# High and low activations as one 512-column operand: three matmuls of 256 columns become one of 512 and one of 256

## The chip, the cores and the metric

One core of a Trainium2 chip runs the whole program in one launch. The metric is the device time in microseconds (us); lower is better. The engines that matter here are TensorE (matmuls, "PE" in the profile, its weight loads "PEld"), VectorE ("DVE"), ScalarE ("ACT"), GpSimd ("POOL") and SyncE ("SP"), which issues the DMAs of the weights.

## The reference, cut to what matters

Two transformer blocks of depth 2 each run over 256 tokens of width 1024. The first block has a mixer with three branches (differential attention, windowed attention, a short convolution), cross attention to a memory of 256 tokens, and a gated network with a convolution of three taps; the second has two gated networks around a mixer. Nearly all the arithmetic is `x @ w` with float32 weights. The gated networks show the form:

```python
def conv_ffn(x, ffn_w_in, ffn_conv_w, ffn_conv_b, ffn_w_out):
    u, gt = jnp.split(x @ ffn_w_in, 2, axis=-1)
    a = dwconv(gt, ffn_conv_w) + ffn_conv_b
    return (jax.nn.silu(a) * u) @ ffn_w_out
...
def swiglu(x, wg, wu, wd):
    return (jax.nn.silu(x @ wg) * (x @ wu)) @ wd
```

Here x is [256, 1024], the inner width is 2816, that is 22 blocks of 128 features.

## The kernel before

**Numbers.** Each float32 value v is held as a pair: a high part h (v rounded to the matmul's format, `F32R`) and a low part v - h. A product is the sum of three matmuls: weight high x activation high, weight high x activation low, weight low x activation high.

**Weights.** They are packed on the host in the order of their use, in halves of [128, 1024]. For each half SyncE issues one DMA of 512 KB into one of 5 staging buffers (`dma_w`, line 296), ScalarE copies it into a high buffer (`split_h`, line 306, 8 buffers), and VectorE subtracts to get the low part (`split_l`, line 318, 7 buffers), which frees the staging buffer and lets the next DMA be issued. `take(key, part)` is called for each half in turn, and calls `pump`, which emits the splits up to 4 halves ahead (low parts) and 5 ahead (high parts). All of this is written out in program order, and each engine runs its instructions in that order.

**Two forms of product.** In form A (`half_A`, `chunk_A`) a [128, 128] weight tile is the stationary operand and the activations xT, [128 features, (high, low), 256 tokens], are the moving one; the result is [128 features, 256 tokens]. One half holds 8 such tiles, one for each slice of the contraction, so it has 8 x 3 = 24 matmuls. A chunk is two halves, whose results lie side by side in one bank of [128, 512]. In the forms B and BK (`group_B`, `group_Bt`, `run_BK`, lines 421 to 501) the activations are stationary and 512 columns of weights move. The change touches form A alone: the keys of cross attention, q and k of the windowed attention, the convolution's projections, the gates and branches of the first mixer, the queries of cross attention, and the up and gate products of all gated networks ("UG", 18 chunks in `ffn1`, 20 in each `swiglu`). In the branches ("A4") a half holds two results of 4 slices each.

**Banks.** Four banks in pool `acc`, four in pool `tp`. The last two chunks of a gated network take theirs from `tp`, since the product behind it needs all four of `acc`.

**Steps.** After each half, `step()` emits work that runs beside the products: attention stages (`attend`), the angle table (`small_setup2`), deferred functions. In `ffn1` the function `gated(j, g, u)` emits for each chunk one activation on ScalarE (line 1238), two multiply-adds on VectorE (1239 and 1240), and, one step later, an activation (1243), a product (1244) and the split of the result (513 on ScalarE, 514 on VectorE). In `swiglu` each chunk has one activation (1336), one product (1337) and the same split. At the start of `ffn1` the chunks c = 0 and 1 ("ffg") have two `gated` each.

Of the kernel before, what the change touches and what calls it, by code (L numbers as in the profile page):

```python
# [11 lines left out]
F32 = mybir.dt.float32  # L12
# [16 lines left out]
HOLD = 4  # L29
NHL = 8  # L30
# [66 lines left out]
def pack_weights(I):  # L97
    """Lays the weights out block by block in the order of their use."""
# [25 lines left out]
    for e in ORDER:  # L124
# [47 lines left out]
# columns of the packed per-feature parameters  # L172
# [16 lines left out]
def pack_rpb(I):  # L189
    """[layer, pair of heads, query, head, key row offset, key column] by index."""  # L190
# [7 lines left out]
def constants():  # L198
    """Tables that the shapes alone determine."""
# [31 lines left out]
class Gen:  # L231
    def __init__(self, nc, tc, T, ctx):
# [9 lines left out]
        self.p_sm = P("sm", 24)  # L242
        PS = bass.MemoryType.PSUM
# [39 lines left out]
    def tp(self):  # L283
        """One of four banks; those of a step are read at the start of the next one."""
# [38 lines left out]
    def pump(self, upto, ahead=1):  # L323
        """High parts up to upto + 1, low parts up to upto."""
# [56 lines left out]
    def mm3(self, out, lh, ll, rh, rl, start, stop):  # L381
        mm = self.nc.tensor.matmul
        mm(out, lh, rh, start=start, stop=False)  # L383
        mm(out, lh, rl, start=False, stop=False)  # L384
        mm(out, ll, rh, start=False, stop=stop)  # L385

    def half_A(self, key, part, out, x, nk=8):
        """out [128 features, 256 tokens]; x(k) gives the pair of k."""
        h, l = self.take(key, part)
        for s in range(8 // nk):  # L390
            for k in range(nk):
                c = (s * nk + k) * 128
                xp = x(k)
                self.mm3(out[:, s, :] if nk < 8 else out, h[:, c:c + 128], l[:, c:c + 128], xp[:, 0, :], xp[:, 1, :],
                         k == 0, k == nk - 1)
# [33 lines left out]
    def group_Bt(self, keys, x, between):  # L429
        """As group_B, with all of token tile 0 ahead of tile 1, whose transposes between() emits."""  # L430
# [109 lines left out]
    def ln_chain(self, xs, g, b):  # L540
        """Layer norm of the two halves xs in place, in parts: what follows each half, and the rest."""
# [16 lines left out]
    def rms_chain(self, xs, g):  # L558
        """As ln_chain, into temporaries."""
# [17 lines left out]
    def both_chain(self, xs, g, b, rg):  # L577
        """Layer norm in place, and the rms norm of it."""
# [8 lines left out]
    def turn_half(self, t, c, half, xT):  # L587
        """half [128 tokens, 512] into xT[:, 4c:4c + 4, :, t]; returns what is left: the low part."""
# [19 lines left out]
    def norm_end(self, keys, x, comb, rows, chain, last=TURN_LAST):  # L608
        """run_BK, the residual, the norm and the transposes of tile 0; returns xT and what is left to do for tile 1."""
# [34 lines left out]
    def turn1(self, halves, xT, late=False):  # L644
        """The transposes of tile 1: f(0) and f(1) by halves unless they come late, f() all that is left."""
# [130 lines left out]
    def mm3_rows(self, outs, rows, q, k, t):  # L776
        """Scores of token tile t: row half i of the pairs q and k into outs[i]."""
# [6 lines left out]
    def heads_unit(self, qT, kT, v, bias, nk, dst, vc, done=None, split=False):  # L784
        """Two heads of 64: qT, kT [128 (two heads), 256], pairs where split; v[kt] [128, cols]; dst their pair."""
# [41 lines left out]
    def first(self, ctx):  # L827
# [21 lines left out]
        self.trig = pf.tile([128, 4, 2, 8], F32, name="trig")  # L849
# [31 lines left out]
        for l in range(DEPTH):  # L881
            xT, tr1 = self.mixer1(l, xT, tr1, pna)
            xT, tr1 = self.cross(l, xT, tr1)
            if l == 0:
                self.sides.append(self.small_setup2())
# [705 lines left out]
```

## Time and profile before

| | us |
|---|---|
| runs, median of 3 | 2078.1 |
| runs, lowest and highest | 2074.76 and 2079.68 |
| profiled execution, span from first to last instruction | 2072.1 |
| TensorE busy in it | 2048.7 |
| VectorE busy | 1302.9 |
| ScalarE busy | 1091.0 |

No time of the profiled execution as a whole stands beside its span; the runs' median is 6.0 us above it. TensorE's granted clock is 0.997 of full speed over the span. Busy time is the union of the instructions on an engine. Matmuls are pipelined, so the duration of one contains the start of the next; the distance between starts tells what one costs in a stream.

### The profile page before, as it was taken

The numbers are of one execution on the slowest core, as the hardware profiler recorded it, in microseconds if no ns is written. First come the engines' busy times: TensorE is split into PE (matmuls) and PEld (weight loads), VectorE is DVE, ScalarE is ACT, GpSimd is POOL, SyncE is SP. The second block draws the span as 40 slices with busy tenths as digits, with TensorE's granted clock in tenths as the row PEclk, the third lists the DMA queues.
The fourth block names the chain that finished last, engine by engine and source line by source line (L and its number), as shares of the span: only waits on it lengthen the run. The fifth ranks groups of instructions, "written<-read, shape, count | busy, mean of one in ns | idle before, by whom it ended". The sixth has DMA issues, their size and how long they took to land.

```text
span 2072.1 us, 34809 instructions
## 1 busy us (share of the span) xinstructions
PE 2048.7 (99%) x14064; PEld 1859.9 (90%) x14064; DVE 1302.9 (63%) x2001; ACT 1091.0 (53%) x1798; POOL 97.0 (5%) x142
## 2 busy tenths in 40 slices
PE   8999999999999999999999999999999999999998
PEld 7899988899888999989987998879998998879996
DVE  6776674887577657457766555776554555676553
ACT  5657445465275644536543544575444544574442
POOL 2100000000010000000001000100000000100000
PEclk9999999999999999999999999999999999999999
DMA  8545664466464465545574656445564656545561
GB/s 290 184 151 169 200 209 135 145 207 217 165 203 138 168 204 180 186 133 188 185 240 160 202 191 218 157 160 169 191 217 142 207 187 217 160 151 178 189 215 66
DMA packets 105523, 376.89 MB, mean 182 GB/s; under 512 B 12561, under 2 KB 12817, under 8 KB 105233
## 3 DMA queue, kind: packets, MB, share of 16 engines
q1 hardware_dynamic: 99936, 357.85, 51.8%
q0 software_dynamic: 5136, 16.29, 2.7%
q8 instruction: 110, 1.80, 0.3%
q10 hardware_dynamic: 288, 0.52, 0.1%
q14 instruction: 53, 0.43, 0.1%
HBM read 372.49 MB, written 1.05 MB: 180 GB/s over the span
## 4 chain that ended last, share of the span: by engine, by line
PE 95%; DVE 3%; issue 1%; ACT 1%; POOL 0%; DMA 0%; SPq 0%; POOLq 0%; DVEq 0%
PE acc L383 17%; PE acc L384 17%; PE acc L385 17%; PE acc L476 6%; PE acc L478 6%; PE acc L477 6%; PE acc L501 5%; PE acc L421 3%; PE acc L423 3%; PE acc L422 3%; PE acc L450 1%; PE acc L443 1%; PE acc L445 1%; PE tp L385 1%; PE tp L383 1%; PE tp L384 1%
## 5 line engine op out<-in xcount | busy, mean ns | idle before, releaser
L318 DVE TENSOR_TENSOR wl<-stg,wh 128x1024 fp32r<-128x1024 f32 x670 | 801.5, 1224 | 196.5 <-PE acc L477 128.4
L306 ACT CAST wh<-stg 128x1024 fp32r<-128x1024 f32 (+1 forms) x673 | 683.3, 1047 | 185.4 <-PE acc L478 133.4
L383 PE MATMUL acc<-xT,wh 128*128 128x256 f32 x2624 | 739.5, 282 | 0.6 <-ACT xT L595 0.6
L384 PE MATMUL acc<-xT,wh 128*128 128x256 f32 x2624 | 735.0, 280 | 0.7 <-DVE xT L596 0.7
L385 PE MATMUL acc<-xT,wl 128*128 128x256 f32 x2624 | 734.9, 280 | 0.0
L383 PEld LDWEIGHTS acc<-xT,wh 128*128 128x128 f32 x2624 | 493.8, 188 | 3.3 <-ACT xT L595 1.1
L384 PEld LDWEIGHTS acc<-xT,wh 128*128 128x128 f32 x2624 | 493.9, 188 | 1.7 <-DVE xT L596 1.1
L385 PEld LDWEIGHTS acc<-xT,wl 128*128 128x128 f32 x2624 | 493.7, 188 | 0.0
L476 PE MATMUL acc<-wh,ring 128*128 128x512 f32 x528 | 212.1, 402 | 0.0
L478 PE MATMUL acc<-wh,ring 128*128 128x512 f32 x528 | 208.3, 395 | 0.2
L477 PE MATMUL acc<-wl,ring 128*128 128x512 f32 x528 | 207.2, 392 | 0.0
L478 PEld LDWEIGHTS acc<-wh,ring 128*128 128x128 f32 x528 | 99.1, 188 | 26.6 <-DVE ring L517 1.1
L477 PEld LDWEIGHTS acc<-wl,ring 128*128 128x128 f32 x528 | 99.2, 188 | 22.8
L501 PE MATMUL acc<-wh,ring 128*128 128x512 f32 x384 | 119.6, 399 | 0.0
L476 PEld LDWEIGHTS acc<-wh,ring 128*128 128x128 f32 x528 | 99.1, 188 | 22.6 <-issue 0.3
L1337 DVE TENSOR_TENSOR tmp<-acc,tmp 128x256 f32<-128x256 f32 x72 | 30.5, 424 | 133.9 <-ACT tmp L1336 133.9
L1336 ACT ACTIVATE tmp<-acc 128x256 f32<-128x256 f32 x72 | 27.7, 385 | 161.6 <-PE acc L385 161.6
L513 ACT CAST ring<-tmp 128x256 fp32r<-128x256 f32 x136 | 54.7, 406 | 87.3 <-DVE tmp L1244 42.0
L514 DVE TENSOR_TENSOR ring<-tmp,ring 128x256 fp32r<-128x256 f32 x136 | 57.3, 425 | 64.1 <-ACT ring L513 64.1
L501 PEld LDWEIGHTS acc<-wh,ring 128*128 128x128 f32 x384 | 72.1, 188 | 16.7
L537 POOL TENSOR_TENSOR sm<-sm,mhalf 128x1 f32<-128x1 f32 (+1 forms) x40 | 31.6, 790 | 1046.4 <-DVE sm L548 418.1
L421 PE MATMUL acc<-wh,xT 128*128 128x512 f32 (+1 forms) x192 | 75.3, 392 | 0.0
(235 smaller groups left out, 2652.3 us busy)
## 6 DMA issues: line engine op xcount, KB each, us to landing
stg<-in_wpack SPq DMA_DIRECT2D x673, 512.0 KB, 4.1
nab<-in_rpb POOLq DMA_DIRECT2D x8, 384.0 KB, 3.7
ring<-in_ln_g POOLq DMA_DIRECT2D x12, 256.0 KB, 3.5
ring<-in_ln_b POOLq DMA_DIRECT2D x12, 256.0 KB, 4.6
ring<-in_ffn_norm POOLq DMA_DIRECT2D x8, 256.0 KB, 4.1
cst<-hpad POOLq DMA_DIRECT2D x32, 32.9 KB, 3.8
ring<-in_memT SPq DMA_DIRECT2D x4, 256.0 KB, 5.9
xn<-in_x SPq DMA_DIRECT2D x4, 256.0 KB, 7.2
```

The costliest lines, as they stand in the source:

```text
L306: self.nc.scalar.copy((h.bitcast(F32) if f32 else h)[:, c:c + w], self.stg[i][:, c:c + w])
L318: (self.nc.gpsimd if i in POOL_LOW else self.nc.vector).tensor_sub(l, s, self.hl[i][0].bitcast(F32))
L383: mm(out, lh, rh, start=start, stop=False)
L384: mm(out, lh, rl, start=False, stop=False)
L385: mm(out, ll, rh, start=False, stop=stop)
L421: mm(o, xp[:, 0, ts], h[:, w], start=(i == 0), stop=False)
L422: mm(o, xp[:, 0, ts], l[:, w], start=False, stop=False)
L423: mm(o, xp[:, 1, ts], h[:, w], start=False, stop=(i == n - 1))
L476: mm(b[t][c], xp[:, 0, ts], h[:, w], start=(i == 0), stop=False)
L477: mm(b[t][c], xp[:, 0, ts], l[:, w], start=False, stop=False)
L478: mm(b[t][c], xp[:, 1, ts], h[:, w], start=False, stop=False)
L501: mm(b[tt][cc], xp[:, 1 if kind == "x" else 0, ts], l[:, w] if kind[0] == "l" else h[:, w], start=False, stop=(kind == "x" and i == n - 1))
```

## The change

In form A the high and the low activations of one slice, which lie next to each other in xT, pass as one moving operand of 512 columns over the high weights; the low weights meet the high activations in a second matmul, which adds into the second half of the bank. The bank then holds weight high x activation high in columns 0 to 255, and the other two terms in 256 to 511. A new function `join` adds the two: ScalarE copies the second half into the destination in SBUF, and VectorE adds the first half to it. So each half (each result of 4 slices in the branches) fills a bank of its own. Consumers that read the bank before now read an SBUF tile, `jn` (a new pool of 2) where no other tile was at hand. The angle table `trig` moves into a buffer of the pool of attention biases `nab`. The comments go.

```diff
-    def mm3(self, out, lh, ll, rh, rl, start, stop):
+    def half_A(self, h, l, c, x, nk, pool):
+        ps = pool()
+        p3 = ps.rearrange("p (a b) -> p a b", a=2)
         mm = self.nc.tensor.matmul
-        mm(out, lh, rh, start=start, stop=False)
-        mm(out, lh, rl, start=False, stop=False)
-        mm(out, ll, rh, start=False, stop=stop)
...
+        for k in range(nk):
+            xp = x(k)
+            w = slice(c + k * 128, c + k * 128 + 128)
+            mm(ps, h[:, w], xp.rearrange("p a b -> p (a b)"), start=(k == 0), stop=False)
+            mm(p3[:, 1, :], l[:, w], xp[:, 0, :], start=False, stop=(k == nk - 1))
+        return p3
+
+    def join(self, out, p3):
+        self.nc.scalar.copy(out, p3[:, 1, :])
+        self.nc.vector.tensor_tensor(out, p3[:, 0, :], out, op=ALU.add)
 
-    def chunk_A(self, key, x, step=True, pool=None):
-        ps = (pool or self.acc)()
-        p3 = ps.rearrange("p (a b) -> p a b", a=2)
+    def chunk_A(self, key, x, outs, step=True, pool=None):
         for s in range(2):
-            self.half_A(key, s, p3[:, s, :], x)
+            h, l = self.take(key, s)
+            self.join(outs[s], self.half_A(h, l, 0, x, 8, pool or self.acc))
             if step:
                 self.step()
-        return p3
...
-            ps = self.chunk_A(("A", "xa_k", l, c), lambda k: self.memT[:, k, :, :])
-            self.nc.scalar.copy(self.KT[:, 2 * c:2 * c + 2, :], ps)
+            self.chunk_A(("A", "xa_k", l, c), lambda k: self.memT[:, k, :, :], [self.KT[:, 2 * c + s, :] for s in range(2)])
...
-                    ps = self.chunk_A(("A", "gate%d" % i, l, 2 * c + j), x)
                     g = self.tmp([128, 2, 256])
-                    nc.scalar.activation(g, ps, AF.Sigmoid)
+                    self.chunk_A(("A", "gate%d" % i, l, 2 * c + j), x, self.two(g))
+                    nc.scalar.activation(g, g, AF.Sigmoid)
...
-                    ps = self.acc().rearrange("p (a b) -> p a b", a=2)
-                    self.half_A(("A4", "br%d" % i, l, c), j, ps, ys[i], nk=4)
+                    ps = self.jn()
+                    w = self.take(("A4", "br%d" % i, l, c), j)
+                    for s in range(2):
+                        self.join(ps[:, s, :], self.half_A(w[0], w[1], 512 * s, ys[i], 4, self.acc))
...
-            ps = self.chunk_A(("UG", "ffn", l, j), x, pool=self.acc if j < NFF - 2 else self.tp)
+            ps = self.jn()
+            self.chunk_A(("UG", "ffn", l, j), x, self.two(ps), pool=self.acc if j < NFF - 2 else self.tp)
             gated(j, ps[:, 1, :], ps[:, 0, :])
```

The other callers of `chunk_A` change in the same manner; in the convolution's first projection the copy out of the bank (`gc`) goes, as the sum is written there.

## Rows read from the trace of the kernel before

**Rows 1.** The page's head and its busy time: engine, us, share, instructions.
```profile
span 2072.1 us, 34809 instructions
PE 2048.7 (99%) x14064; PEld 1859.9 (90%) x14064; DVE 1302.9 (63%) x2001; ACT 1091.0 (53%) x1798; POOL 97.0 (5%) x142
```
**Rows 2.** TensorE's waits by cause: us in total, times, longest.
```profile
PE acc L383 <- ACT wh L306: 5.4, 1, 5.4
PE tp L591 <- DVE tmp L573: 2.7, 1, 2.7
PE acc L385 <- DVE wl L318: 1.4, 1, 1.4
...
PE tp L803 <- DVE sm L739: 0.3, 1, 0.3
```
**Rows 3.** Groups of line 383 by shape: count | busy us, mean ns.
```profile
L383 PE MATMUL acc<-xT,wh 128*128 128x256 f32 x2624 | 739.5, 282 | 0.6 <-ACT xT L595 0.6
...
L383 PEld LDWEIGHTS acc<-xT,wh 128*128 128x128 f32 x2624 | 493.8, 188 | 3.3 <-ACT xT L595 1.1
...
L383 PE MATMUL acc<-ring,wh 128*128 128x256 f32 x192 | 54.4, 283 | 0.0
...
L383 PE MATMUL tp<-xT,wh 128*128 128x256 f32 x192 | 53.7, 280 | 0.0
...
L383 PE MATMUL acc<-memT,wh 128*128 128x256 f32 x128 | 38.1, 298 | 5.5 <-ACT wh L306 5.4
```
**Rows 4.** TensorE's timeline, second block's first gated network: start us, us.
```profile
1141.54 0.36 PE L383 MATMUL acc<-xT,wh 128*128 128x256 f32 x1
...
1248.63 0.40 PE L476 MATMUL acc<-wh,ring 128*128 128x512 f32 x1
```
**Rows 5.** TensorE's timeline in the full-width product behind it.
```profile
1262.64 0.40 PE L476 MATMUL acc<-wh,ring 128*128 128x512 f32 x1
...
1285.74 0.40 PE L476 MATMUL acc<-wh,ring 128*128 128x512 f32 x1
```
**Rows 6.** Groups on ScalarE and VectorE by shape: count | busy us, mean ns | idle.
```profile
L513 ACT CAST ring<-tmp 128x256 fp32r<-128x256 f32 x136 | 54.7, 406 | 87.3 <-DVE tmp L1244 42.0 <-DVE tmp L1337 39.5 <-DVE tmp L1117 5.7
...
L1337 DVE TENSOR_TENSOR tmp<-acc,tmp 128x256 f32<-128x256 f32 x72 | 30.5, 424 | 133.9 <-ACT tmp L1336 133.9
...
L1336 ACT ACTIVATE tmp<-acc 128x256 f32<-128x256 f32 x72 | 27.7, 385 | 161.6 <-PE acc L385 161.6
...
L1238 ACT ACTIVATE tmp<-acc,cols 128x256 f32<-128x256 f32 x40 | 22.5, 563 | 29.7 <-PE acc L385 25.0 <-DVE tmp L1240 4.7
...
L513 ACT CAST ring<-tp 128x256 fp32r<-128x256 f32 x48 | 17.8, 370 | 39.9 <-PE tp L1177 17.3 <-PE tp L803 9.2 <-PE tp L1326 6.4
```
**Rows 7.** VectorE's timeline in ffn1 of layer 0, one chunk.
```profile
442.77 0.48 DVE L1239 SCALAR_TENSOR_TENSOR tmp<-acc,cols,tmp 128x255 f32<-128x255 f32 x1
...
446.04 1.22 DVE L318 TENSOR_TENSOR wl<-stg,wh 128x1024 fp32r<-128x1024 f32 x1
447.18 0.48 DVE L1239 SCALAR_TENSOR_TENSOR tmp<-acc,cols,tmp 128x255 f32<-128x255 f32 x1
```
**Rows 8.** Timelines of TensorE and VectorE in ffn1 of layer 0.
```profile
392.52 0.37 PE L383 MATMUL acc<-xT,wh 128*128 128x256 f32 x1
...
413.42 0.48 DVE L1239 SCALAR_TENSOR_TENSOR tmp<-acc,cols,tmp 128x255 f32<-128x255 f32 x1
...
458.17 0.48 DVE L1239 SCALAR_TENSOR_TENSOR tmp<-acc,cols,tmp 128x255 f32<-128x255 f32 x1 [1.13 <-ACT tmp L1238]
```
**Rows 9.** The same in ffn1 of layer 1.
```profile
944.35 0.37 PE L383 MATMUL acc<-xT,wh 128*128 128x256 f32 x1
...
963.25 0.48 DVE L1239 SCALAR_TENSOR_TENSOR tmp<-acc,cols,tmp 128x255 f32<-128x255 f32 x1
```
**Rows 10.** All waits: us in total, times, longest.
```profile
ACT tmp L1336 <- PE acc L385: 161.6, 68, 2.5
...
ACT tmp L1238 <- PE acc L385: 25.0, 22, 1.2
```

More of the change, by code (lines that the diff above doesn't have):

```diff
@@ L29 @@
 HOLD = 4
+JN = 2
 NHL = 8
@@ L242, in __init__ @@
         self.p_sm = P("sm", 24)
+        self.p_jn = P("jn", JN)
         PS = bass.MemoryType.PSUM
@@ L378, in drain, with jn, two @@
             self.step()
-    def mm3(self, out, lh, ll, rh, rl, start, stop):
+    def half_A(self, h, l, c, x, nk, pool):
+        ps = pool()
+        p3 = ps.rearrange("p (a b) -> p a b", a=2)
         mm = self.nc.tensor.matmul
-        mm(out, lh, rh, start=start, stop=False)
-        mm(out, lh, rl, start=False, stop=False)
-        mm(out, ll, rh, start=False, stop=stop)
[L387 to L395, printed above, removed]
-    def chunk_A(self, key, x, step=True, pool=None):
-        ps = (pool or self.acc)()
-        p3 = ps.rearrange("p (a b) -> p a b", a=2)
+        for k in range(nk):
[8 more added lines that the diff above has]
+    def chunk_A(self, key, x, outs, step=True, pool=None):
         for s in range(2):
-            self.half_A(key, s, p3[:, s, :], x)
+            h, l = self.take(key, s)
+            self.join(outs[s], self.half_A(h, l, 0, x, 8, pool or self.acc))
             if step:
                 self.step()
-        return p3
+    def jn(self):
+        return self.p_jn.tile([128, 2, 256], F32, tag="jn", name=self.nm("jn"))
+    def two(self, t):
+        return [t[:, 0, :], t[:, 1, :]]
     def group_B(self, keys, x, step=True, ncol=512):
@@ L848, in first @@
         load_x(1)
-        self.trig = pf.tile([128, 4, 2, 8], F32, name="trig")
         self.posf = pf.tile([128, 2], F32, name="posf")
@@ L884, in first @@
             if l == 0:
+                t = pna.tile([128, 2, 384], F32, tag="nab", name=self.nm("nab"))
+                self.trig = t[:, 0, :64].rearrange("p (a b c) -> p a b c", a=4, b=2)
                 self.sides.append(self.small_setup2())
@@ L1065, in mixer1 @@
             for n, lst, scale in (("qb", qbT, 0.125), ("kb", kbT, 1.0)):
-                ps = self.chunk_A(("A", n, l, c), x)
+                ps = self.jn()
+                self.chunk_A(("A", n, l, c), x, self.two(ps))
                 for s in range(2):
@@ L1104, in mixer1 @@
         for c in range(2):
-            ps = self.chunk_A(("A", "gc", l, c), x)
             gc = self.tmp([128, 2, 256])
-            nc.scalar.copy(gc, ps)
-            ps = self.chunk_A(("A", "hc", l, c), x)
+            self.chunk_A(("A", "gc", l, c), x, self.two(gc))
+            ps = self.jn()
+            self.chunk_A(("A", "hc", l, c), x, self.two(ps))
             nc.vector.tensor_tensor(gc, ps, gc, op=ALU.mult)
@@ L1115, in mixer1 @@
                 nc.vector.scalar_tensor_tensor(y[:, s, :255], gc[:, s, 1:], w(2), y[:, s, :255], op0=ALU.mult, op1=ALU.add)
-            ps = self.chunk_A(("A", "gb", l, c), x)
+            ps = self.jn()
+            self.chunk_A(("A", "gb", l, c), x, self.two(ps))
             nc.vector.tensor_tensor(y, ps, y, op=ALU.mult)
@@ L1134, in mixer1 @@
                 for j in range(2):
-                    ps = self.chunk_A(("A", "gate%d" % i, l, 2 * c + j), x)
                     g = self.tmp([128, 2, 256])
-                    nc.scalar.activation(g, ps, AF.Sigmoid)
+                    self.chunk_A(("A", "gate%d" % i, l, 2 * c + j), x, self.two(g))
+                    nc.scalar.activation(g, g, AF.Sigmoid)
                     gs.append(g)
                 for j in range(2):
-                    ps = self.acc().rearrange("p (a b) -> p a b", a=2)
-                    self.half_A(("A4", "br%d" % i, l, c), j, ps, ys[i], nk=4)
+                    ps = self.jn()
+                    w = self.take(("A4", "br%d" % i, l, c), j)
+                    for s in range(2):
+                        self.join(ps[:, s, :], self.half_A(w[0], w[1], 512 * s, ys[i], 4, self.acc))
                     self.step()
@@ L1195, in q @@
         def q(h):
-            ps = self.chunk_A(("A", "xa_q", l, h), x)
+            ps = self.jn()
+            self.chunk_A(("A", "xa_q", l, h), x, self.two(ps))
             t = self.ring([128, 2, 256])
@@ L1271, in ffn1 @@
         for c in range(2):
-            g = self.chunk_A(("A", "ffg", l, c), x)
+            g = self.jn()
+            self.chunk_A(("A", "ffg", l, c), x, self.two(g))
             for s in range(2):
@@ L1275, in ffn1 @@
         for j in range(4, NFF):
-            ps = self.chunk_A(("UG", "ffn", l, j), x, pool=self.acc if j < NFF - 2 else self.tp)
+            ps = self.jn()
+            self.chunk_A(("UG", "ffn", l, j), x, self.two(ps), pool=self.acc if j < NFF - 2 else self.tp)
             gated(j, ps[:, 1, :], ps[:, 0, :])
@@ L1331, in swiglu @@
         for j in range(2, NFF):
-            ps = self.chunk_A(("UG", n, l, j), x, pool=self.acc if j < NFF - 2 else self.tp)
+            ps = self.jn()
+            self.chunk_A(("UG", n, l, j), x, self.two(ps), pool=self.acc if j < NFF - 2 else self.tp)
             if j == 2:
@@ L1469, in mixer2 @@
         for c in range(2):
-            ps = self.chunk_A(("UG", "cv", l, c), x)
+            ps = self.jn()
+            self.chunk_A(("UG", "cv", l, c), x, self.two(ps))
             s = self.tmp([128, 256])
```

## Prediction

> **What bounds the kernel now.** I read the page's busy shares first: TensorE is busy for 2048.7 us of a span of 2072.1 us [rows 1]. Then who made TensorE wait: nine causes, the longest 5.4 us once at the start, the next 2.7 us once at the end, the rest 1.4 us or less [rows 2]. So TensorE's stream of matmuls is the time, and a change can win only by shortening that stream and lose only by making it wait. Busy time overlaps from one matmul to the next, so a matmul's price is not its 280 ns but the distance between two starts. I took that from the timeline over long stretches: in the first gated network of the second block, 19 chunks of 48 matmuls of 256 columns lie between two starts at 1141.54 and 1248.63 us [rows 4], which is 107.09/912 = 117.42 ns each. In the full-width product behind it, 99 matmuls of 512 columns lie between 1262.64 and 1285.74 us [rows 5], 233.33 ns each. The reader is to see that twice the columns cost 1.987 times the time: a matmul here is paid by its columns, and almost nothing by the piece.
>
> **What the change does on TensorE.** For each of the 8 (or 4) slices of the contraction, three matmuls of 256 columns become one of 512 and one of 256. The columns are the same 768. Before: 3 x 117.42 = 352.26 ns. After: 233.33 + 117.42 = 350.75 ns, 1.51 ns less. Line 383 counts the slices: 2624 + 192 + 192 + 128 = 3136 [rows 3], so the gain is 3136 x 1.51 = 4.7 us. No row shows the two lengths in turn, so I bound it: if the 512-column pass keeps the small surplus of the short ones (2 x 117.42 = 234.84) the gain is nothing; if the short pass loses it too (half of 233.33, 116.67) a slice takes 350.0 ns and the gain is 7.1 us. I take 4.7, the direct sum. A third of the weight loads go as well. They last 188 ns each at a spacing of 117 [rows 3], so they run beside the matmuls, and the spacing already goes by the columns; I cost their loss at nothing, beyond what the bounds hold.
>
> The Trainium skill, page "TensorE: Matmul & The Clock Gate", section "Back-to-back issue gap", gives a spacing of columns / 2.4 GHz plus 2.5 ns for each matmul. By it a slice would fall from 327.5 to 325.0 ns, an estimated gain of 7.8 us. The rows do not agree with its level (117.42 and 233.33 ns against 109.2 and 215.8), and the piece price that solves both rows is 2 x 117.42 - 233.33 = 1.51 ns.
>
> **What it adds on ScalarE and VectorE.** The bank now holds two halves that must be summed: one ScalarE copy of 256 columns (385 ns by the nearest row, line 1336) and one VectorE addition (424 ns, line 1337) for each output [rows 6]. There are 2624/8 + 192/8 + 128/8 + 192/4 = 328 + 24 + 16 + 48 = 416 of them: 160 us more on ScalarE and 176 us more on VectorE, less a dozen copies (the KT and gc ones) that go. Both engines stay under three quarters of the span on average; what matters is where it is not average.
>
> Three other effects come with it. Each half takes its own bank, so the four banks last for 4 halves, not 8: a sum must be done 3 halves (3 x 8 x 350.75 ns = 8.4 us) after its matmuls. ScalarE's copy now waits for TensorE's end at every half, not every second one; behind it on ScalarE stand the step's attention work and the next weight split, behind VectorE's addition the next low part. The low part of half i+4 is asked for at half i and needed 11.2 us later, and the DMA that refills its staging buffer is five halves ahead, so neither is late as long as VectorE lags by less than the banks allow. Moving the small angle table onto a spare bias buffer costs nothing: that buffer's attention is over, and the next layer's bias load on POOL comes after the table's last use.
>
> **Where the cover is thin.** In the second block's gated networks it holds: ScalarE waited for TensorE at 68 of the 72 activations of line 1336 [rows 10], so both engines were caught up; a chunk there gains 0.85 us of additions in 5.6 us. In the first block's convolved network (ffn1) it does not: only 22 of line 1238's 40 activations [rows 6] waited for TensorE [rows 10]. There VectorE's work goes to and fro with ScalarE. When it is behind, one chunk takes it 447.18 - 442.77 = 4.41 us [rows 7]; caught up, it shows as 1.13 us idle ahead of line 1239 [rows 8]. The change puts into this cycle: the first addition behind a weight split, 0.34 us net (an instruction that waits for nothing starts some 0.08 us before the end of the one ahead, as 446.04 + 1.22 against 447.18); the second one in full, 0.42 + 0.04; and line 1238 can no longer start on the bank ahead of VectorE but waits for that addition, so 0.57 + 0.04 us of ScalarE stand inside the cycle. That is 4.41 + 0.34 + 0.46 + 0.61 = 5.82 us, plus 0.04 because line 1238 reads SBUF where it read a bank (line 513: 406 against 370 ns [rows 6]): 5.86 us. TensorE's chunk is 16 x 350.75 ns = 5.61 us. VectorE falls behind by 0.25 us a chunk and never recovers before the full-width product.
>
> How far it may fall: line 1239 stands 0.65 us behind the addition that frees the bank, so TensorE stops when that line is 8.4 + 0.65 = 9.1 us late. In layer 0 the second half started at 392.52 us, so chunk 4 ended near 392.52 + 5 x 2.82 = 406.6, and its line 1239 came at 413.42 us [rows 8]: already 6.8 us late, because of the transposed first chunks and the angle table. Three chunks of additions at about 0.8 us (part of the new wait falls into old ones) use up the room. So 17 chunks x 0.25 = 4.2 us stall, and the table's remaining VectorE work adds between 0 and 3 us (I take 0.8, most of it falls into the new waits): 5.0 us. In layer 1, 944.35 + 14.1 = 958.4 against 963.25 us [rows 9] is 4.8 us late, about 7.4 with the additions; the remaining 1.7 last 6 to 7 chunks, and the other 12 x 0.25 = 3.0 us stall. Together 8 us; from 3 (round trips hide half of the 0.25) to 12.
>
> In the mixers and the cross attention, scores and their readers are one step apart, and the readers now stand behind a copy that waits for TensorE. The nearest row is the attention wait of 0.3 us in the list of TensorE's waits [rows 2]; nothing excludes more. I take 2 us for some sixteen units, from 0 to 6.
>
> **Sum.** -4.7 + 8 + 2 = +5.3 us on a span of 2072.1 us: 2077.4. The median of the runs shown lies 6.0 us above that span, which gives 2083.4 us, 0.26% slower. About 0.2% (4 us) is what a measurement here can tell from no change.
>
> **Rivals.** (1) It cancels: the additions hide better than I think (half of the 8 us, none of the 2), and the gain is 4.7: 2078.1 - 4.7 + 4 = 2077.4 us. For it: the kernel's deep lead of four halves. Against: line 1239's lateness, which was there before. (2) Faster: the cost goes by the matmul and not by the column, the full 7.1 us by the lower bound of the short pass, with no stall in ffn1: 2071 us. It decides if VectorE's cycle in ffn1 stays below 5.61 us. Against it: the 1.987. By the rule of the Trainium skill quoted above the same case would be 2070.3 us. (3) Attention too: the copy's wait moves each stage of an attention unit half a step to one step on, and TensorE, in order, waits 1 us at a dozen of the units: 12 us there and 8 in ffn1 less 4.7, 2093 us. It decides where a unit's norm ends later than 2.8 us after its step. For it: ScalarE's burst of exponentials; against: hardly a wait of this kind before.
>
> **How the numbers follow.** The forecast (VectorE sets the pace of ffn1) has 0.50, with a range of its own of 2080 to 2089; cancelling 0.27; faster 0.15; attention too 0.08. The first lies above +0.2% in seven eighths (0.44); with the last that is 0.52 slower. The rest of it and the second give 0.33 same, and 0.15 is faster. The range that leaves out no more than 2 in 10 reaches into the faster case by half and up to the edge of the last: 2071 to 2091.
>
> **What would show it.** Right: line 383's matmul has 512 columns and its successor starts 233 ns later, the short one 117 ns; TensorE waits for VectorE's addition (bank release) at every second half in ffn1, by about 0.25 us, and nowhere in the second block; ffn1's chunks are 5.8 to 5.9 us long and the second block's 5.61. Wrong: a spacing of the pair clearly under 350 ns; no TensorE wait in ffn1; or waits of several us in the attention steps.

## The result, and the profile after

The changed kernel takes 2113.2 us (median of 5 runs, 2111.2 to 2113.7), the kernel before 2077.5 us beside it (5 runs). The ratio is 1.0172, 95% interval [1.0161, 1.0184]: 1.7% slower. The forecast was slower too, but 2083.4 us with a range up to 2091, so it is 30 us too low and the time lies outside its range.

The page of after, its head and busy time, answers to [rows 1]:

```profile
span 2111.4 us, 29071 instructions
PE 2050.5 (97%) x10928; PEld 1713.5 (81%) x10928; DVE 1452.3 (69%) x2417; ACT 1214.3 (58%) x2202; POOL 97.1 (5%) x142
```

TensorE has 3136 matmuls fewer and is busy as long as before, in a span 39.3 us longer. ScalarE and VectorE gained 123 and 149 us and are still far from full. TensorE's idle time grew from 23.4 to 60.9 us, so nearly all of the added time is time in which TensorE stood. The waits of TensorE in after (cause: us in total, times, longest), beside [rows 2]:

```profile
PE acc L392 <- DVE jn L398: 14.1, 5, 3.3
PE acc L392 <- DVE memT L522: 5.8, 1, 5.8
PE tp L599 <- DVE tmp L581: 5.3, 2, 2.8
PE tp L762 <- DVE tmp L1032: 5.1, 4, 2.0
PE tp L762 <- ACT tmp L725: 5.1, 2, 4.2
PE tp L789 <- ACT ring L524: 2.1, 4, 0.9
PE acc L393 <- DVE wl L320: 2.1, 3, 1.5
...
PE acc L453 <- DVE wl L320: 2.0, 1, 2.0
```

Line 392 is the matmul of 512 columns, 393 the short one, 397 and 398 the copy and the addition of a join; 762 and 789 are the transposes and scores of the attention, 1032 its combination of two heads. Of the kernel before, only the 5.8 us at the start (5.4 there) and about half of line 599's are old. New are the waits for the join itself (14.1) and for the attention's own tiles (12.3). The two lines on line 320, the split that makes the low part of a weight, are 4.1 us, all in the first 40 us; before had 1.4 us of this kind (line 318 in [rows 2]).

The matmuls and the joins by group (count | busy us, mean ns of one | idle time before), beside [rows 3] and [rows 6]:

```profile
L392 PE MATMUL acc<-xT,wh 128*128 128x512 f32 x2624 | 928.3, 397 | 16.5 <-DVE jn L398 14.1 <-DVE xT L604 2.0
...
L398 DVE TENSOR_TENSOR jn<-acc,jn 128x256 f32<-128x256 f32 x320 | 132.7, 419 | 112.8 <-ACT jn L397 112.8
...
L397 ACT COPY jn<-acc 128x256 f32<-128x256 f32 x320 | 116.0, 367 | 140.9 <-PE acc L393 140.4
```

The pieces of these 320 joins cost about what was forecast, 367 and 419 ns for 385 and 424. The last column is the point: the copy spent 140 us at the head of ScalarE's queue waiting for TensorE, the addition 113 us at the head of VectorE's waiting for the copy. Over all kinds of joins, 79 us of the copies' waits lie in the two mixers; most of the rest lies where TensorE loses nothing by it. Of the 140.9 us only 0.5 were for anything but TensorE, so no wait for one of the two buffers of `jn` shows.

TensorE's timeline in the second block's first gated network (start us, us), answering to [rows 4]:

```profile
1188.16 0.39 PE L392 MATMUL acc<-xT,wh 128*128 128x512 f32 x1
...
1293.21 0.40 PE L484 MATMUL acc<-wh,ring 128*128 128x512 f32 x1
```

Between the two lie 303 slices: 105.05/303 = 346.7 ns each, where before had 352.3 and the forecast 350.75.

**Where the span went.** I cut TensorE's timeline where its lines pass from one kind of product to the next; 71 stretches come out, the same in every run here, and their lengths repeat between runs to a few hundredths of a us where nothing differs. In groups, us:

| stretches | before | after | difference |
|---|---|---|---|
| start, memory keys, first full-width product | 47.5 | 51.5 | +4.0 |
| mixer of layer 0 | 242.3 | 263.5 | +21.2 |
| mixer of layer 1 | 241.2 | 259.3 | +18.1 |
| cross attention and full-width products by it, both layers | 220.7 | 219.4 | -1.3 |
| ffn1 and the products behind it, both layers | 368.9 | 372.7 | +3.8 |
| second block to its last product | 879.6 | 873.1 | -6.5 |

The six rows add up to 39.3, the difference of the spans, and the two mixers of the first block are as much as the whole; the rest cancels. (The start is 46.5 to 47.5 us long in every run here that has the memory keys in the old form, and 48.5 to 52.7 in those that have them in the new one.)

**One of their gaps.** TensorE, ScalarE and VectorE of after in the branches of layer 0's mixer:

```profile
192.09 0.28 PE L393 MATMUL acc<-ring,wl 128*128 128x256 f32 x1
195.63 0.50 PE L392 MATMUL acc<-xT,wh 128*128 128x512 f32 x1 [3.27 <-DVE jn L398]
...
186.21 0.37 ACT L397 COPY tmp<-acc 128x256 f32<-128x256 f32 x1 [2.13 <-PE acc L393]
...
187.60 1.28 ACT L751 ACT_TABLE_LOAD   x1
190.04 0.47 ACT L751 ACTIVATE tmp<-tp,sm 128x256 f32<-128x256 f32 x1 [1.16 <-DVE sm L749]
...
191.99 1.28 ACT L1147 ACT_TABLE_LOAD   x1
193.29 0.63 ACT L1147 ACTIVATE tmp<-tmp 128x512 f32<-128x512 f32 x1
193.82 1.03 ACT L308 CAST wh<-stg 128x1024 fp32r<-128x1024 f32 x1
194.76 0.64 ACT L397 COPY jn<-acc 128x256 f32<-128x256 f32 x2
...
195.16 0.76 DVE L398 TENSOR_TENSOR jn<-acc,jn 128x256 f32<-128x256 f32 x2 [3.22 <-ACT jn L397]
```

ScalarE first stands 2.13 us for a product (186.21), so the attention's work behind it begins late: table load, exponentials (line 751), table load, sigmoid of the gates (1147), a weight split. Only then, 7.2 us after the first table load, come the copies (194.76) whose additions (195.16) free two banks. A branch's half has 4 slices, 1.4 us, so the four banks last 5.5 us; TensorE ran out of them behind the matmul of 192.09 and stood 3.27 us. The Trainium skill, page "PSUM — Partial Sum Buffer", section "Engine vs sequencer instructions", says that the queues of ScalarE and VectorE are strictly first in, first out; the trace agrees, the copies at 194.76 stand behind exponentials, two table loads and a weight split that have nothing to do with their banks.

**And the clock.** Windows of after (us; busy us of PE, PEld, DVE, ACT, POOL with counts; granted clock; DMA share, GB/s):

```profile
215.00:220.00 5.00, 1.76 (x8) 1.31 (x7) 1.45 (x7) 4.30 (x9) 0.00 (x0) 0.82 0.28 105
220.00:225.00 5.00, 5.00 (x19) 4.33 (x18) 5.00 (x9) 3.52 (x8) 0.00 (x0) 0.50 0.28 83
225.00:230.00 5.00, 5.00 (x31) 4.42 (x30) 3.32 (x5) 2.79 (x5) 0.00 (x0) 1.00 0.71 224
```

TensorE was busy 1.76 of 5 us, then worked 5 us at a granted clock of 0.50, the lower level (1.2 in place of 2.4 GHz), with 19 matmuls where the next window, at full clock, has 31. Over the span the clock is 0.992 against 0.997, that is 2 x 2111.4 x 0.008 = 34 us at the lower level against 12; at most half of the difference, 11 us, is lost to it. Nearly all of it is part of the mixers' 39 us: over their two stretches the clock is 0.97 and 0.98, where before has 1.00, and TensorE's busy time is 10.5 us above before's although its stream is shorter.

### The profile page after: what moved, and what is told of

It is laid out like the page before. It is cut to its first block, busy times and chain, and to the rows that moved or that the text cites. A ratio compares the mean times of both kernels' runs of the same rounds, so it can differ in the third digit from the quotient of the medians.

```text
span 2111.4 us, 29071 instructions
## 1 busy us (share of the span) xinstructions
PE 2050.5 (97%) x10928; PEld 1713.5 (81%) x10928; DVE 1452.3 (69%) x2417; ACT 1214.3 (58%) x2202; POOL 97.1 (5%) x142
## 4 chain that ended last, share of the span: by engine, by line
PE 83%; DVE 8%; ACT 5%; issue 2%; DMA 1%; POOL 1%; POOLq 0%; SPq 0%; DVEq 0%; ACTq 0%
PE acc L392 27%; PE acc L393 13%; PE acc L484 6%; PE acc L485 6%; PE acc L486 6%; PE acc L509 5%; PE acc L429 3%; PE acc L431 2%; PE acc L430 2%; PE tp L392 2%; DVE wl L320 2%; PE acc L458 1%; PE acc L453 1%; PE acc L451 1%; ACT tmp L751 1%
## 5 line engine op out<-in xcount | busy, mean ns | idle before, releaser
L392 PE MATMUL acc<-xT,wh 128*128 128x512 f32 x2624 | 928.3, 397 | 16.5 <-DVE jn L398 14.1
L320 DVE TENSOR_TENSOR wl<-stg,wh 128x1024 fp32r<-128x1024 f32 x670 | 814.5, 1226 | 142.0 <-PE acc L485 104.4
L308 ACT CAST wh<-stg 128x1024 fp32r<-128x1024 f32 (+1 forms) x673 | 696.5, 1048 | 160.0 <-PE acc L486 112.4
L392 PEld LDWEIGHTS acc<-xT,wh 128*128 128x128 f32 x2624 | 496.5, 189 | 133.0 <-DVE jn L398 21.1
L398 DVE TENSOR_TENSOR jn<-acc,jn 128x256 f32<-128x256 f32 x320 | 132.7, 419 | 112.8 <-ACT jn L397 112.8
L397 ACT COPY jn<-acc 128x256 f32<-128x256 f32 x320 | 116.0, 367 | 140.9 <-PE acc L393 140.4
L603 ACT CAST xT<-tp 128x512 fp32r<-128x512 f32 x48 | 27.7, 588 | 90.7 <-PE tp L599 90.4
L429 PE MATMUL acc<-wh,xT 128*128 128x512 f32 (+1 forms) x192 | 75.6, 394 | 0.0
L431 PE MATMUL acc<-wh,xT 128*128 128x512 f32 (+1 forms) x192 | 72.3, 376 | 0.0
```

Of the source, the lines that this page charges most:

```text
L308: self.nc.scalar.copy((h.bitcast(F32) if f32 else h)[:, c:c + w], self.stg[i][:, c:c + w])
L320: (self.nc.gpsimd if i in POOL_LOW else self.nc.vector).tensor_sub(l, s, self.hl[i][0].bitcast(F32))
L392: mm(ps, h[:, w], xp.rearrange("p a b -> p (a b)"), start=(k == 0), stop=False)
L397: self.nc.scalar.copy(out, p3[:, 1, :])
L398: self.nc.vector.tensor_tensor(out, p3[:, 0, :], out, op=ALU.add)
L429: mm(o, xp[:, 0, ts], h[:, w], start=(i == 0), stop=False)
```

## The experiments

In the runs that mix the forms, the old form has its own functions (three matmuls of 256 columns, a bank for two halves, no join), and a set names the stages that have the new one: xk and xq keys and queries of the cross attention, qk, conv, gate, br the parts of the mixer, ffn1, swiglu and cv (the second block). Lines 393 and 394 (in e3 393 to 395, none of them longer than 256 columns, and in e5 394 and 395) are then the new form's matmuls.

| run | us | ratio to before, 95% interval |
|---|---|---|
| e1 second block alone new | 2068.1 | 0.9956 [0.9941, 0.9970] |
| e2 mixers old | 2074.3 | 0.9989 [0.9979, 0.9998] |
| e3 512 issued as two of 256 | 2124.9 | 1.0228 [1.0213, 1.0243] |
| e4 joins behind the step | 2092.1 | 1.0071 [1.0056, 1.0086] |
| e5 work kept, banks old | 2269.7 | 1.0935 [1.0919, 1.0952] |
| e6 banks alone | 2090.0 | 1.0069 [1.0054, 1.0084] |
| e7 joins on VectorE | 2116.2 | 1.0190 [1.0173, 1.0207] |
| e8 branches old | 2096.4 | 1.0100 [1.0085, 1.0115] |
| e9 work on own buffers | 2092.2 | 1.0086 [1.0071, 1.0101] |
| e10 banks alone, readers late | 2075.3 | 1.0003 [0.9994, 1.0013] |
| e11 joins late, branches old | 2080.8 | 1.0030 [1.0018, 1.0041] |
| e12 new where it pays | 2064.7 | 0.9956 [0.9939, 0.9973] |
| e13 as e9, behind the step | 2090.5 | 1.0071 [1.0054, 1.0088] |
| e14 ffn1 old | 2111.2 | 1.0168 [1.0153, 1.0184] |
| e15 as e9, uncoupled | 2079.9 | 1.0022 [1.0013, 1.0032] |
| e16 ScalarE's work alone | 2074.0 | 0.9991 [0.9982, 1.0000] |
| e17 VectorE's work alone | 2078.0 | 1.0010 [1.0001, 1.0020] |

The kernel before had medians of 2074.4 to 2077.5 us beside them. e5, e6, e9, e10, e13 and e15 to e17 change the mixers only and are read against e2.

**Where: e1 and e2.**

```diff
-STAGES = {"xk", "qk", "conv", "gate", "br", "xq", "ffn1", "swiglu", "cv"}
+STAGES = {"swiglu", "cv"}                          (e1)
+STAGES = {"xk", "xq", "ffn1", "swiglu", "cv"}      (e2)
```

> The new form stands only in the four gated feed-forward stretches and the strided convolutions of the second block (176 of the 416 joins); all of the first block has the three products of 256 columns and one bank per chunk, as before. Theory M (the loss is in the first block's mixers, where the joins stand among the attention's work on ScalarE and VectorE and hold the banks): each of the four stretches shows 111.4 us in place of 113.1, nothing waits, so 4 times 1.76 and some 0.7 us for the convolutions come off: 2077.5 - 7.7 = 2070. Rival W (the joins cost by their work alone, wherever they stand: the loss of 36 us and the 17 us of matmul gain spread over 416 joins, 0.127 us each): 22 - 7.7, 2092.

> The new form everywhere but in the two mixers of the first block, which have the old one (136 of the 416 joins are left out). Theory M: second block -7.7, cross attention some -2.4, first feed-forward +4.2 as its stretches in the trace of after (longer by 2.84 + 0.75 in one layer, by 0.6 in the other): 2077.5 - 5.9 = 2072. Rival W (work alone): 280 joins at 0.127 us are +35, 2240 of 3136 slices give back 12: 2100. The recorded forecast's reason (the first feed-forward is the main loss): the loss of 36 us is nearly all still there, 2105 to 2113.

Measured 2068.1 and 2074.3. In e1 each of the four gated stretches fell from 113.15 to 111.39 us. In e2 the mixers' stretches are 242.3 and 241.3 us, before's own lengths, and all the other stretches are as in after. So the 39 us between e2 and after come with the new form in the mixers, with its 136 joins and their banks; the other 280 together cost less than their matmuls gain. Theory W, a price per join wherever it stands, falls, and so does the forecast's reason that ffn1 is the main loss.

**What the gain is of: e3.**

```diff
-            mm(ps, h[:, w], xp.rearrange("p a b -> p (a b)"), start=(k == 0), stop=False)
+            mm(p3[:, 0, :], h[:, w], xp[:, 0, :], start=(k == 0), stop=False)
+            mm(p3[:, 1, :], h[:, w], xp[:, 1, :], start=False, stop=False)
```

> As after, banks and joins and all, but the product of 512 columns is issued as two of 256 columns, one into each half of the bank. It tells what the gain on TensorE is of (346.7 ns per slice in the trace of after, 352.3 before). Theory 512 (it is one instruction fewer): 352 ns per slice come back, the gated feed-forward stretches show 113.1 us, the time is some 12 to 17 us above after, 2125 to 2130. Rival C (it is that matmuls in succession write different columns): 347 ns stay, 111.4 us, 2113.

Measured 2124.9, 11.7 above after, and 113.15 us for each gated stretch. So the 5.6 ns a slice are those of one matmul fewer, together with its weight load; the two were not taken apart. In the mixers and ffn1, where other engines set the pace, part of it is not to be had: hence 12 us and not 3136 x 5.6 ns = 17.5.

**Order: e4.** In the mixers' whole-width chunks (there `late` is true) the step's attention work is emitted ahead of the join:

```diff
-            self.join(outs[s], self.half_A(h, l, 0, x, 8, pool or self.acc))
-            if step:
+            p = self.half_A(h, l, 0, x, 8, pool or self.acc)
+            if step and self.late:
+                self.step()
+            self.join(outs[s], p)
+            if step and not self.late:
                 self.step()
```

> As after, but in the first block's mixers the join of a half of a whole-width chunk is emitted behind the next step's attention work on ScalarE and VectorE, not ahead of it. Theory B (the banks are held too long because their readers stand behind attention work): the banks are held one step longer, TensorE's waits for the join's addition grow from 14 us, the time is 2118 or more. Rival O (the joins push the attention's own work back, and TensorE waits for that): the waits of transposes and scores for the attention's tiles (some 17 us over all) shrink to half or less, and the time is 2100 or less.

Measured 2092.1: 21 us of the 39 are the order. The waits for the attention's tiles shrink from 12.3 to about 5 us (lines 762 and 789 are 792 and 819 here); the join's are split in two groups and stay:

```profile
PE acc L393 <- DVE jn L423: 7.1, 5, 1.5
...
PE acc L393 <- DVE tmp L423: 5.5, 4, 2.4
...
PE tp L792 <- ACT tmp L755: 3.1, 1, 3.1
...
PE tp L792 <- DVE tmp L1066: 1.4, 2, 0.7
```

So rival O holds, not theory B: what a join ahead of the step costs is that the attention's work stands behind it.

**Work and banks apart: e5 and e6.** e5 has the old products and banks and keeps a copy and a VectorE operation of the same size at each join's place; e6 has the banks and no joins.

```diff
+    def join_W(self, out, p):                                      (e5)
+        self.nc.scalar.copy(out, p)
+        self.nc.vector.tensor_tensor(out, p, out, op=ALU.max)
...
+    def halves_O(self, key, x, use):                               (e6)
+        for s in range(2):
+            h, l = self.take(key, s)
+            p = self.acc()[:, :256]
+            self.half_O(p, h, l, 0, x, 8)
+            use(s, p)
+            self.step()
```

> All as after but the first block's mixers, where the work of the joins is kept and their banks are not: three products of 256 columns, both halves of a result in one bank as before, and still a ScalarE copy and a VectorE operation (a maximum of the copy and its source, which changes nothing) at each of the 136 places. To be read beside the second experiment (mixers as before, 2074.3) and after (2113.2). Theory W (the added work in the queues is the loss, it pushes the attention's steps back): nearly all of the 39 us between these two are there, 2105 or more. Theory B (the banks, of which each half now takes a whole one, are the loss): 2076 to 2082.

> The other part alone: three products of 256 columns in the first block's mixers, each half in a bank of its own, and no joins there; the operation that uses a result reads each half by itself, in the join's place. To be read beside 2074.3 (second experiment) and 2113.2 (after). Theory B: most of the 39 us are there, 2100 or more. Theory W: 2074 to 2080. If both parts are needed (a bank is only short when its reader stands behind other work), this and the run before lie both well under half of the loss, 2076 to 2088 each.

e5 missed its question. Its waits of TensorE:

```profile
PE acc L403 <- DVE jn L417: 108.0, 34, 8.1
PE acc L403 <- DVE tmp L417: 20.0, 22, 1.4
```

Line 403 is the first product of a half; it waits for the readers of the half before it in the same bank, 128 us. The Trainium skill, page "PSUM — Partial Sum Buffer", section "PSUM bank collisions raise a hardware error", says that accesses of two engines to the same bank and quarter of the partitions are to be kept apart by semaphores whatever the columns, and that guarding by the whole bank is the simple version. The trace agrees: TensorE stood for the readers of the other half of the columns, and the 128 us are what that cost here. Two halves in one bank are good only if both are read after the second.

e6 is 2090.0, 16 us over e2 and outside the ranges of all three theories, and no wait for a bank of the mixers is among its causes. What TensorE waits for are the attention's tiles (795, 822 and 844 are lines of the attention):

```profile
PE tp L844 <- DVE sm L780: 3.1, 2, 2.5
...
PE tp L795 <- DVE tmp L1068: 2.6, 2, 1.3
```

**Which engine: e7 and e8.**

```diff
-        self.nc.scalar.copy(out, p3[:, 1, :])                      (e7; on_dve in the mixers)
+        if self.on_dve:
+            self.nc.vector.tensor_copy(out, p3[:, 1, :])
+        else:
+            self.nc.scalar.copy(out, p3[:, 1, :])
...
-STAGES = {"xk", "qk", "conv", "gate", "br", "xq", "ffn1", "swiglu", "cv"}
+STAGES = {"xk", "qk", "conv", "gate", "xq", "ffn1", "swiglu", "cv"}   (e8)
```

> As after, but the joins of the first block's mixers run wholly on VectorE (it copies the one half from the bank and adds the other to it), so that none of them stands in ScalarE's queue behind exponentials and table loads. Theory A (ScalarE's queue holds the joins): the waits for the join's addition fall from 14 us to a few, 2095 or less. Theory V (VectorE's queue is as late): VectorE has some 0.42 us more at each of 136 places, the waits stay or grow, 2113 or more.

> As after, but the products of the branches in the mixers (half of a result every 1.4 us, 48 of the 416 joins) have the old form. Theory S (a short half makes the four banks too few, so the branch stretches are the loss themselves): their 7.9 us in each layer and the 4 to 5 us of the stretches right behind them go, 2113 - 24 = 2089. Rival L (the engines are late by then from the stretches before, and TensorE waits as long at another place): 2105 or more.

e7: 2116.2, nothing won, which is theory V's time; the waits for the banks fell nonetheless, as theory A had it. Its waits of TensorE show why:

```profile
PE tp L792 <- DVE tmp L1066: 11.8, 8, 2.3
PE acc L514 <- DVE jn L426: 7.4, 2, 3.7
...
PE acc L393 <- DVE jn L426: 2.7, 5, 1.1
```

The banks of the chunks and branches are freed sooner (2.7 us in place of 14.1), and the attention's combination on VectorE is late instead (11.8 for 5.1), as is the last join ahead of the mixer's full-width product. e8: 2096.4, 17 of the 39 us, between its two theories. The branch stretches lose nearly all their excess, and the gates' stretches behind them keep a part of theirs (14.6 us for 13.8 in before).

**Work by itself: e9, e13, e15, e16 and e17.** The old mixers, and in each join's place work of its size on buffers of its own.

```diff
+    def work(self, d):                                             (e9; e13 after the step)
+        if self.dummy:
+            self.nc.scalar.copy(d[:, 1, :], d[:, 0, :])
+            self.nc.vector.tensor_tensor(d[:, 1, :], d[:, 0, :], d[:, 1, :], op=ALU.add)
...
+            self.nc.scalar.copy(d[0][:, 1, :], d[0][:, 0, :])          (e15, e16)
+            self.nc.vector.tensor_tensor(d[1][:, 1, :], d[1][:, 0, :], d[1][:, 0, :], op=ALU.add)   (e15, e17)
```

> All as after but the first block's mixers, which have the old products and readers; in the place of each of their 136 joins stand a ScalarE copy and a VectorE addition of 256 columns that read and write a buffer of their own in SBUF, so that they take their queues' time, wait for no product and hold no bank. They change no result. To be read beside 2074.3 (second experiment, the same without them) and 2113.2 (after). Theory W (the work alone): 2100 or more. Theory O (what costs is not the work but that a join, standing ahead of the attention's work, makes its queue wait for TensorE, and standing behind it, holds a bank): 2074 to 2080.

> The ninth experiment (work like that of the joins on buffers of its own, 2092.2) with each piece of work emitted behind the next step's attention work, and behind the pair of halves in the branches. The same number of operations of the same kind. Theory O (the place ahead of the attention's steps is the price): 2074 to 2079, as the second experiment without any such work. Theory W (the amount): 2088 or more.

> The ninth experiment (2092.2) with the two engines' extra work uncoupled: ScalarE copies within a buffer of its own, VectorE adds within another, so that neither waits for the other or for a product; number, size and place of the operations are the same. Theory C (in the ninth and thirteenth runs ScalarE's copy waited for VectorE's addition before it, 32 and 30 us in all, and this coupling of the two queues is the price): 2074 to 2080. Theory W (the queues' time alone): 2088 or more.

> The run before with ScalarE's copies alone (136 of 405 ns, 55 us of its time). Theory A (ScalarE, where the attention's exponentials and table loads stand, is what the work delays): at least two thirds of what the run before loses against 2074.3. Theory V (VectorE, where its norms stand): a third or less.

> The same with VectorE's additions alone (136 of 421 ns, 57 us). Theory A: a third or less of the loss of the uncoupled run. Theory V: two thirds or more. If each alone costs next to nothing and both together do, the loss is of the chain that passes from one queue to the other.

e9 came out at 2092.2 and e13 at 2090.5, between the theories of e9 and with W in e13: 16 to 18 us, wherever the work stands. But the groups of e9 show that this is not plain work:

```profile
L410 ACT COPY jn<-jn 128x256 f32<-128x256 f32 x136 | 55.1, 405 | 32.3 <-DVE jn L411 32.2
...
L411 DVE TENSOR_TENSOR jn<-jn 128x256 f32<-128x256 f32 x136 | 57.2, 421 | 53.4 <-ACT jn L410 52.9
```

Each copy waits for the addition before it, each addition for its copy; the two queues go in step. Uncoupled (e15) the same operations show

```profile
L410 ACT COPY jn<-jn 128x256 f32<-128x256 f32 x136 | 55.1, 405 | 0.8
...
L411 DVE TENSOR_TENSOR jn<-jn 128x256 f32<-128x256 f32 x136 | 60.4, 444 | 0.8
```

and cost 5.6 us in all (2079.9; 6.6 us by the mixers' stretches): theory C. ScalarE's share is nothing (e16, 2074.0), VectorE's 3.7 us (e17, 2078.0), which is the two thirds of theory V. The two shares fall 2 us short of both together, no more than the intervals leave open.

**Banks without the order, and both cures: e10 and e11.**

```diff
-            use(s, p)                                              (e10, on e6)
             self.step()
+            use(s, p)
```

> The sixth experiment (each half in its own bank, old products, no joins, 2090.0) with each half's reader emitted behind the next step's attention work, not ahead of it. Theory O (the 16 us of that run are the order): 2074 to 2079. Theory B (they are the banks): 2088 or more, with waits for the readers of the banks in it.

> The fourth experiment (joins behind the step, 2092.1) with the branches' products in the old form, as in the eighth. If the two parts of the loss are apart (order in the whole chunks, short halves in the branches), the branch stretches' excess of that run goes as well (4.2 and 2.1 us in each layer, 12.7 in all, by its trace): 2079 to 2081. If what the one takes away turns up again at the other's place: 2086 or more.

e10 is 2075.3, 1.0 above e2 with overlapping intervals (the mixers' stretches are 0.7 us longer in all): the halved banks by themselves cost nothing here, and 15 of e6's 16 us were the readers' place. e11, the joins behind the step and the branches in the old form, is 2080.8, as summed from the parts; the two cures are apart.

**ffn1 by itself: e14.** The set without ffn1.

> As after, but the first feed-forward of both layers has the old form. It measures the forecast's term for it by itself: 8 us of TensorE's standing still, of which the cheaper products give some 3.5 back (640 slices of 5.5 ns), so that the old form should be 4.5 us faster here, 2113.2 - 4.5 = 2108.7. If VectorE didn't limit these stretches in after, the old form is slower by the products' gain: 2116.7.

Measured 2111.2, 2.0 below after, which the two intervals do not tell from nothing. The stretches do, since they repeat to hundredths: ffn1 with the product behind it is 2.4 us shorter than after's in layer 0 and 0.6 longer in layer 1, 1.8 in all. It is less than the 4.5 expected because the old form here takes 114.80 us a stretch and not the 113.56 of before (see the end).

**What pays: e12.** The set is xq, swiglu, cv, and in the mixers the gates get the new form only where the attention is over:

```diff
-                    if "gate" in STAGES:
+                    if i == 0 or (i == 1 and c == 1):
```

> The new form only where the stretches of the runs so far were shorter with it: the second block (8.3 us under before in the first experiment), the queries of the cross attention (2.3 us by the stretches of after), and the last three pairs of gates of each mixer, behind the attention's work (0.29 us each, 1.8 in all); the branches, the first feed-forward and all else as before. Sum: 2076.4 - 8.3 - 2.3 - 1.8 = 2064. Rival: a gate's join held up by what is left of the attention, 2068 or more.

Measured 2064.7, a ratio of 0.9956 [0.9939, 0.9973], faster than both kernels. Its span is 2061.7 us against 2066.3 of e1, and the gates' stretches show the 0.29 us each; but by the ratio e1 is as good, and the two cannot be told apart by times.

## Why the prediction was wrong

**The step that failed** is the last term of the sum: "In the mixers and the cross attention ... I take 2 us for some sixteen units, from 0 to 6." The cross attention was right (it gains 1.3 us and hardly waits); the mixers lost 39 us net. That the change was forecast to be slower, and is, is luck: the forecast's loss was ffn1's, and with the mixers in the old form (e2) the change is no slower than before. The nearest row, one wait of 0.3 us in [rows 2], told how the attention stood with its readers behind its own work, and the change moved just that. The mechanism was named, as rival 3 (the copy waits for TensorE at the head of ScalarE's queue, the attention's stages move on), and given 12 us and a chance of 0.08. Here is what the runs show of it:

- The order. The same joins behind the step's work cost 21 us less (e4), and readers of single halves, without any join, 15 us less (e10 against e6). A wait for TensorE at the head of an in-order queue is paid by all that stands behind it; for work that waits for no product the place was worth 1.7 us (e13 against e9).
- The branches. The room of the banks ("a sum must be done 3 halves", 8.4 us) was worked out from halves of 8 slices. In the branches a half has 4, so the room is 4.2 us, and ScalarE's burst of exponentials with two table loads of 1.28 us is 7.2 us long in the gap shown. With the branches in the old form 17 us are gone (e8), and with this and the order (e11) 32 of the 39.
- The rest, 6.5 us of e11 over e2, is of the size of what the work alone costs (e15, 5.6 us, mostly VectorE's). That it is that work is not shown: e11 has 88 of the 136 joins, and its shorter stream of matmuls gives something back. Up to 11 us of the 39 passed through the lower clock behind the gaps; no run takes the clock apart from the waits that brought it.

How much of the loss hangs on the chain from ScalarE's copy to VectorE's addition stays open: e9 against e15 shows 12 us for tying two queues to each other, but there each copy waits for an addition on VectorE, which a join's copy does not. In after it is the reader of a sum that makes ScalarE wait: the sigmoid of the gates (line 1147) waited 8.1 us for the joins' additions, where in before it read the bank. No run takes this wait apart.

**The gain on TensorE** had the right mechanism and the wrong size: 350.75 ns a slice, a gain of 4.7 us, bounds to 7.1. It measured 346.7 ns, 5.6 below before, which is 17.5 us over 3136 slices where nothing else sets the pace (e1 got 8.3 us by the medians with the second block alone, 7.0 us by its four gated stretches). The lower bound of 350.0 took the full-width product's 233.33 ns [rows 5] for the least a pass of 512 columns can cost; next to short passes it costs less (in the second block's first gated network the short pass starts 229.5 ns after the long one on average). The prediction also put the loss of a third of the weight loads at nothing, and no run shows whether that holds. By the rule of the Trainium skill quoted in the prediction, which the page gives for the isolated gap of one matmul and not for a stream, a matmul fewer is worth 2.5 ns; the runs show 5.6.

**ffn1** was right in its mechanism and its pace, and in its total partly by luck. VectorE's cycle was forecast at 5.86 us a chunk; TensorE in layer 0 of after:

```profile
460.64 0.50 PE L392 MATMUL acc<-xT,wh 128*128 128x512 f32 x1 [1.11 <-DVE jn L398]
...
466.48 0.51 PE L392 MATMUL acc<-xT,wh 128*128 128x512 f32 x1
...
472.32 0.50 PE L392 MATMUL acc<-xT,wh 128*128 128x512 f32 x1
...
501.54 0.50 PE L392 MATMUL acc<-xT,wh 128*128 128x512 f32 x1
```

The starts are 5.84 us apart, five chunks long once more (29.22/5). At the free pace (111.39 us a stretch as in the second block, and 0.4 for two more transposes) the two stretches would be 111.8 us; they are 116.40 and 113.40, and the products behind them 0.8 and 0.3 longer: 7.3 us of standing, where 5.0 + 3.0 were forecast. But only nine chunks of layer 0 and five of layer 1 are near 5.84 us long, where 17 and 12 were to stall: both layers stall later than forecast, and the last chunk runs free. Layer 0 makes up for it with the one wait of 1.11 us and the product behind it. The standing falls on both halves of a chunk (2.88 and 2.96 us for 2.77), not on every second one.

**The rest.** No wait for a join came up in the second block, as forecast; TensorE's one longer wait there, 2.6 us at 1174.82 us, is at the transposes ahead of the first gated network. The low parts of the weights were forecast in time and were not, at the start: the 2.0 us of line 453 are part of the start's 4.0 us. The rest of these was not followed up. The 2.7 us that the prediction read in [rows 2] as "at the end" stand at 1118.77 us, where the first block passes to the second. Of what was to show the prediction wrong, two things came: a pair clearly under 350 ns, and waits of several us in the attention's steps.

## What to carry to other kernels

Before a reader is put into an in-order queue, list what stands behind it and who waits for that: here the place of the joins was worth 21 us and their work on the engines 6. Work out a buffer's room for the shortest user of it, not for the usual one. And apply such a change by stages: where the queues were free it paid (e1, e12), and where bursts of other work share them it cost more than four times what it paid in the second block.

## What was not expected of the hardware

- A matmul of 512 float32 columns costs 233 ns in a stream of its kind [rows 5], and a pair of 512 and 256 columns 346.7 ns, so that the pair is 4 ns below the sum of the two streams' prices.
- The old form of ffn1 ran at two paces with the same instructions: 113.56 us a stretch in before and in layer 0 of e12, 114.80 in e1 and e14 and 114.77 in layer 1 of e12, without a wait that the profile shows. The cause was not sought.
- After TensorE had been busy 1.76 of 5 us, the next 5 us ran at a granted clock of 0.50. But after the gap of 3.27 us at 192 us, no shorter than the one in that window (3.24 us), the clock stayed at 1.00.
